# Splitting weights two blocks at a time, unscaled, with the norms' gains moved to the activations

## The chip, the core and the metric

The kernel runs on one core of a Trainium2 chip. That core has a matrix engine (TensorE, here PE), three engines for elementwise work (VectorE or DVE, ScalarE or ACT, GpSimd or POOL), a queue for transfers (SyncE or SP) and 16 DMA engines. An engine runs its instructions in the order in which they stand in its queue and waits on semaphores for the others. The metric is the time of one execution on the device in microseconds; the median of three runs before the change is 967.39 us (966.79 to 967.49).

## The reference

A trunk of two layers works on 256 tokens of 1024 features in float32. Each layer has three sub-layers, and each sub-layer has a root-mean-square norm before it and another behind it:

```python
for l in range(DEPTH):
    f = swiglu(rms_norm(x, ffn1_pre_g[l]), ffn1_w_gu[l], ffn1_w_down[l])
    x = x + 0.5 * rms_norm(f, ffn1_post_g[l])
    m = hybrid_mixer(rms_norm(x, mix_pre_g[l]), mix_w_in[l], mix_w_out[l], ...)
    x = x + rms_norm(m, mix_post_g[l])
    f = swiglu(rms_norm(x, ffn2_pre_g[l]), ffn2_w_gu[l], ffn2_w_down[l])
    x = x + 0.5 * rms_norm(f, ffn2_post_g[l])
```

`swiglu` multiplies by a 1024 x 5632 matrix, forms silu(g) * u and multiplies by a 2816 x 1024 one. `hybrid_mixer` multiplies by a 1024 x 2566 matrix; the result goes through three groups of heads (a gated linear recurrence, a Mamba-2 state space model in two chunks of 128 tokens, called SSD, whose result is normed with a gain of its own, `ssd_norm_g`, and a causal gMLP), and their 1024 columns are multiplied by `mix_w_out`. A norm is `rms_norm(x, g) = x * rsqrt(mean(x*x) + eps) * g`. The gain `g` belongs to a feature, that is, to a row of the weight that follows.

## The kernel before

**Products.** Every float32 operand of a main product is split into a high part (rounded to the type float32r of the language) and a low part (operand minus high part). A product is three matmuls, high x high, high x low and low x high, into one PSUM bank. `mm3` (L420) issues the three with 512 (or 390) weight columns as the moving operand and 128 tokens as the stationary one; `b_tile` (L692) issues them with 128 weight columns stationary and all 256 tokens moving.

**Weights.** All weights come in one packed stream. A unit is one block of 128 rows and up to 512 columns; there are 656 of them, in the order of use (`weight_units`, L51). Units are loaded in chunks of four (the first three chunks have one, one and two) into three staging buffers over SP's queue (`dma_chunk`, L339). A unit is then split (`split_next`, L383): ACT writes the high part and DVE the low part into a slot of two times 512 columns. There are 17 slots of kind "w"; a few general ones of kind "a" (13 in all) may be lent to the weights when a sub-layer allows it (`extra`). A unit's slot comes free with its last product (`release`, L413).

**Gains.** The pre-norm's gain is multiplied into the weight during the split, since a gain belongs to a weight row and a row to a partition: a unit that follows a norm is split by L400 (ACT, with a scale) and L401 (DVE, multiply and subtract), another by L396 and L397. So the norm's operand is x itself, transposed. `1 / rms` goes to the results. The same is done with `ssd_norm_g` for three of the eight row blocks of `mix_w_out`.

**From one sub-layer to the next.** `post` (L533) takes a token tile's two result banks: squares on ACT, gain on DVE (into tiles `s_f`, of which there are three), `1 / rms` by a power on POOL, and x is brought up to date on DVE. `pre` (L569) then makes the next operand for that token tile in two halves: four transposes on PE into a bank, a cast to the high part on ACT, a subtraction for the low part on DVE (tile `nT`). Down-products of the last four (or five) row blocks are held back, so that the first token tile ends earlier and its `post` and `pre` run beside the second tile's last products. In the first block of a sub-layer the first token tile's products come before the second's.

**What sets the order.** The program is written by a planner. It steps along PE's main products with a clock of its own for every engine (`T`), in which each operation costs a fixed part and a part by columns. The side computations are generators (`Chain`, L110), whose operations are issued when the planner holds their inputs to be due; all helpers of a chain issue at L137. `fill` (L364) issues splits of weights whenever DVE and ACT are due within 0.6 us and a slot is free. Thus every edit of an operation's cost can change the order of all engines' queues. `keep` pins the order of the first 15 us.

**Mixer.** Its first 16 units are the columns for dt and z (390 wide) and for the gMLP (512); then come groups of 384 or 512 columns for gates, recurrence, B and C, and x of the SSD; the out-product is last. `ssd_chunk` (L1092) norms the SSD's result without its gain, transposes it, and `split_out` (L869) writes the two parts.

Of the kernel before, what the change touches and what calls it, by code (L numbers as in the profile page):

```python
# [23 lines left out]
NSLOT = 17  # L24
NSCR = 13
# [25 lines left out]
def weight_units():  # L51
    units = []

    def add(name, l, blocks, scale=None):
        units.append((name, l, blocks, scale))

    def ffn(l, w):
        gu, dn, pg = f"ffn{w}_w_gu", f"ffn{w}_w_down", f"ffn{w}"
        for b in range(5):
            for off in (0, DFF):  # L60
                for k in range(KT):
                    add(gu, l, [(k * P, off + b * 512, 512)], (pg, k))
        for k in range(KT):
            add(gu, l, [(k * P, 2560, 256), (k * P, DFF + 2560, 256)], (pg, k))
        for k in range(DKT):
            for n in range(2):
                add(dn, l, [(k * P, n * 512, 512)])

    for l in range(DEPTH):
        ffn(l, 1)  # L70
        for k in range(KT):
            add("mix_w_in", l, [(k * P, C_DT, 6), (k * P, C_Z, 384)], ("mix", k))
        for k in range(KT):
            add("mix_w_in", l, [(k * P, C_UV, 512)], ("mix", k))
        for grp in FGROUPS:
            for k in range(KT):
                add("mix_w_in", l, [(k * P, c, P) for _, _, c in grp], ("mix", k))
        for k in OUT_KTS:
            for n in range(2):
                add("mix_w_out", l, [(k * P, n * 512, 512)], ("norm", k - 3) if 3 <= k < 6 else None)  # L80
# [4 lines left out]
def weight_chunks(units):  # L85
# [6 lines left out]
    return chunks  # L92

# [16 lines left out]
class Chain:  # L110
    """A side computation: a generator whose operations are issued when their inputs are due."""
# [110 lines left out]
class Kernel:  # L222
    def __init__(self, ctx, tc, x, wts, pf, pb, gpost, wst, wri, out):
# [20 lines left out]
        self.chunks = weight_chunks(self.units)  # L244
        self.u2c = {}
# [12 lines left out]
        self.wt, self.wh, self.wready, self.slot_time = {}, {}, {}, {}  # L258
        self.extra, self.keep_free = 0, 4

    # ---------------------------------------------------------------- memory
# [30 lines left out]
    # ---------------------------------------------------------------- issue order  # L292
# [25 lines left out]
    def wait_for(self, cond):  # L318
        while True:
# [4 lines left out]
            if self.next_split < len(self.units):  # L324
# [13 lines left out]
    # ---------------------------------------------------------------- weights  # L338
# [18 lines left out]
    def fill_time(self):  # L357
        d = self.next_split
        ci, _ = self.u2c[d]
# [4 lines left out]
    def fill(self):  # L364
        did = False
        while self.next_split < len(self.units):
            d = self.next_split
            ci, _ = self.u2c[d]
# [14 lines left out]
    def split_next(self, kind):  # L383
        d = self.next_split
        nc, T = self.nc, self.T
        u = self.units[d]
        w = unit_width(u)
        ci, o = self.u2c[d]
        src = self.ctile[ci][:, o:o + w]
        t, h = self.get([P, 2, 512], F32R, kind)  # L390
        hi, lo = t[:, 0, :w], t[:, 1, :w]
        sc = u[3] is not None
        T["act"] = max(T["act"], self.carrive[ci], self.slot_time.get(h, 0.0) + HOP) + 0.095 + w * 0.000833 + 0.095 * sc
        T["dve"] = max(T["dve"], T["act"] + HOP) + 0.07 + 0.06 * sc + w * 0.00104
        if not sc:
            self.keep(nc.scalar.copy(hi, src))  # L396
            self.keep(nc.vector.tensor_tensor(out=lo, in0=src, in1=hi.bitcast(F32), op=ALU.subtract))  # L397
        else:
            s = self.pcol(u[1], u[3][0], u[3][1])
            self.keep(nc.scalar.activation(hi, src, AF.Copy, scale=s))  # L400
            self.keep(nc.vector.scalar_tensor_tensor(out=lo, in0=src, scalar=s, in1=hi.bitcast(F32),  # L401
# [797 lines left out]
```

## Time and profile before

| | |
|---|---|
| median of the runs | 967.39 us (966.79 to 967.49) |
| span of the profiled execution, first to last instruction | 963.5 us |
| median less span | 3.9 us |
| PE busy | 945.1 us, 98% |
| DVE busy | 649.1 us, 67% |
| ACT busy | 580.4 us, 60% |
| POOL busy | 40.1 us, 4% |
| granted PE clock, mean | 0.998 |
| read from HBM | 173.57 MB, 181 GB/s over the span |

The profiled execution has no other time of its own than its span; what lies around the span is taken from the timed runs. Groups are named by line, engine, operation and tiles (written <- read). `acc` is a PSUM bank, `s_w` a weight slot, `s_a`, `s_m` and `s_f` are general tiles, `stg` is a staging buffer, `pf` the table of gains and other columns. PEld is PE's loading of stationary operands. The windows give for each stretch its length, the busy time of PE, PEld, DVE, ACT and POOL with the number of instructions, the granted clock, the share of the DMA engines' time and GB/s. With one line chosen, a window gives that line's busy time alone. In the timeline a row begins with start and length; in square brackets is idle time ahead of it and what ended it.

### The profile page before, as it was taken

The page shows a single profiled execution, that of the slowest core. Times are in us where ns is not written, and L with a number is a line of the kernel's source. Part 1 is how long each engine was busy: PE and PEld are TensorE (multiplying, and loading weights), DVE is VectorE, ACT ScalarE, POOL GpSimd, SP SyncE. Part 2 cuts the span into 40 slices and gives each one's busy share as a digit, 9 for nine tenths or more (in the row PEclk, how much of TensorE's full clock was granted, in tenths as well). Part 3 has the DMA queues.
Part 4 walks back from the last instruction along what each step waited for, and adds up shares of the span by engine and source line. Part 5 has one row for each costly group of instructions (what it writes and reads, how often), then busy time and mean ns, then how long its engine had stood idle before and what let it go on. Part 6 is the DMA issues. An engine that isn't in the chain of part 4 may idle for free.

```text
span 963.5 us, 16052 instructions
## 1 busy us (share of the span) xinstructions
PE 945.1 (98%) x6292; PEld 862.9 (90%) x6292; DVE 649.1 (67%) x1169; ACT 580.4 (60%) x1057; POOL 40.1 (4%) x58
## 2 busy tenths in 40 slices
PE   7999999999999999999999999999999999999997
PEld 6999998889986999998889999888999779999885
DVE  5876666566899856676565666666588996566632
ACT  7865555576967765555564555555589685454531
POOL 1100000001001100000010000000010110000000
PEclk9999999999999999999999999999999999999999
DMA  8855555443246945566435555663431566455621
GB/s 309 290 202 205 188 208 208 154 168 116 88 136 212 327 165 175 176 218 221 172 130 198 175 183 209 221 224 113 177 127 45 206 231 236 137 193 210 214 80 44
DMA packets 26717, 175.66 MB, mean 182 GB/s; under 512 B 2960, under 2 KB 3344, under 8 KB 7824
## 3 DMA queue, kind: packets, MB, share of 16 engines
q1 hardware_dynamic: 24768, 169.93, 50.0%
q10 hardware_dynamic: 1872, 4.70, 1.4%
q8 instruction: 49, 0.80, 0.3%
q14 instruction: 28, 0.23, 0.1%
HBM read 173.57 MB, written 1.05 MB: 181 GB/s over the span
## 4 chain that ended last, share of the span: by engine, by line
PE 89%; DVE 6%; ACT 2%; POOL 1%; issue 1%; DMA 0%; DVEq 0%; POOLq 0%; ACTq 0%
PE acc L704 46%; PE acc L425 39%; PE acc L137 4%; DVE s_w L401 2%; DVE s_a L137 1%; ACT s_a L137 1%; DVE x L137 1%; DVE s_f L137 1%; POOL postr L137 1%; DVE nT L137 1%; ACT L137 1%; POOL rs L137 0%; DMA x<-in_x_dram 0%; ACT junk L137 0%; POOL lnr L137 0%
## 5 line engine op out<-in xcount | busy, mean ns | idle before, releaser
L704 PE MATMUL acc<-nT,s_w 128*128 128x256 f32 x3900 | 467.5, 279 | 0.0
L704 PEld LDWEIGHTS acc<-nT,s_w 128*128 128x128 f32 x3900 | 460.3, 188 | 0.7
L401 DVE SCALAR_TENSOR_TENSOR s_w<-stg,pf,s_w 128x512 fp32r<-128x512 f32 (+2 forms) x435 | 299.2, 735 | 112.8 <-ACT s_w L400 112.5
L400 ACT ACTIVATE s_w<-stg,pf 128x512 fp32r<-128x512 f32 (+2 forms) x435 | 279.4, 701 | 113.7 <-PE acc L704 62.1
L425 PE MATMUL acc<-s_w,s_a 128*128 128x512 f32 x984 | 227.4, 390 | 0.0
L425 PEld LDWEIGHTS acc<-s_w,s_a 128*128 128x128 f32 x984 | 184.1, 188 | 37.9
L397 DVE TENSOR_TENSOR s_w<-stg,s_w 128x512 fp32r<-128x512 f32 x184 | 121.9, 687 | 61.9 <-ACT s_w L396 61.7
L396 ACT CAST s_w<-stg 128x512 fp32r<-128x512 f32 x184 | 107.0, 619 | 68.6 <-PE acc L425 36.7
L425 PE MATMUL acc<-s_w,nT 128*128 128x512 f32 (+1 forms) x522 | 129.3, 394 | 1.2 <-DVE nT L137 1.0
L425 PEld LDWEIGHTS acc<-s_w,nT 128*128 128x128 f32 x522 | 95.7, 189 | 21.6 <-DVE nT L137 2.3
L137 ACT ACTIVATE s_m<-s_m 128x512 f32<-128x512 f32 x36 | 22.6, 632 | 79.9 <-DVE s_m L137 79.9
L137 DVE TENSOR_TENSOR s_m<-acc,s_m 128x512 f32<-128x512 f32 (+1 forms) x64 | 35.7, 562 | 31.3 <-PE acc L704 25.8
L425 PE MATMUL acc<-s_w,s_m 128*128 128x512 f32 x192 | 48.0, 399 | 0.0
L425 PEld LDWEIGHTS acc<-s_w,s_m 128*128 128x128 f32 x192 | 34.8, 188 | 7.0 <-ACT s_m L137 0.5
L137 POOL TENSOR_TENSOR postr<-postv,mhalf 128x1 f32<-128x1 f32 x12 | 10.7, 893 | 705.7 <-DVE postv L137 705.7
L137 ACT CAST s_a<-s_m 128x512 fp32r<-128x512 f32 x36 | 22.1, 615 | 27.4 <-DVE s_m L137 26.9
L137 DVE TENSOR_TENSOR s_f<-acc,gp 128x512 f32<-128x512 f32 x24 | 16.5, 687 | 32.9 <-ACT junk L137 32.9
L137 ACT ACTIVATE junk<-acc 128x512 bf16<-128x512 f32 x24 | 14.2, 594 | 38.7 <-PE acc L425 38.2
L137 DVE TENSOR_TENSOR s_m<-acc,rb 128x512 f32<-128x512 f32 x36 | 24.7, 687 | 14.4 <-PE acc L704 14.4
L137 DVE TENSOR_TENSOR s_a<-s_m,s_a 128x512 fp32r<-128x512 f32 x36 | 24.7, 687 | 10.0 <-ACT s_a L137 10.0
L137 DVE SCALAR_TENSOR_TENSOR s_a<-s_f,pf,s_a 128x255 f32<-128x255 f32 (+2 forms) x60 | 28.5, 496 | 3.9 <-ACT s_a L137 3.9
L704 PE MATMUL acc<-nT,s_a 128*128 128x256 f32 x180 | 26.8, 279 | 0.0
(130 smaller groups left out, 526.0 us busy)
## 6 DMA issues: line engine op xcount, KB each, us to landing
stg<-in_wts_dram SPq DMA_DIRECT2D x147, 1024.0 KB, 5.0
stg<-in_wts_dram SPq DMA_DIRECT2D x12, 768.0 KB, 4.3
stg<-in_wts_dram SPq DMA_DIRECT2D x4, 780.0 KB, 4.4
gp<-in_gpost_dram ACTq DMA_DIRECT2D x6, 512.0 KB, 5.7
x<-in_x_dram SPq DMA_DIRECT2D x2, 512.0 KB, 4.4
out_dram<-x SPq DMA_DIRECT2D x4, 256.0 KB, 2.0
pb<-in_pb_dram ACTq DMA_DIRECT2D x2, 265.0 KB, 5.2
stg<-in_wts_dram SPq DMA_DIRECT2D x2, 256.0 KB, 4.6
```

Source lines behind the costliest of these rows:

```text
L137: ins = fn(*args, **kw)
L396: self.keep(nc.scalar.copy(hi, src))
L397: self.keep(nc.vector.tensor_tensor(out=lo, in0=src, in1=hi.bitcast(F32), op=ALU.subtract))
L400: self.keep(nc.scalar.activation(hi, src, AF.Copy, scale=s))
L401: self.keep(nc.vector.scalar_tensor_tensor(out=lo, in0=src, scalar=s, in1=hi.bitcast(F32), op0=ALU.mult, op1=ALU.subtract))
L425: self.keep(mm(out, a, b, start=start and i == 0, stop=stop and i == 2))
L704: self.keep(self.nc.tensor.matmul(out, a, b, start=k == 0 and i == 0, stop=k == KT - 1 and i == 2))
```

## The change

A group is two neighbouring units of a chunk (`split_groups`); the first two units, which have chunks of their own, are groups of one. `split_next` splits a whole group with one ACT copy and one DVE subtraction of up to 1024 columns, and never scales. High and low part have a slot of 1024 columns each, so a group takes two slots; 16 "w" slots stand in place of 17, and 14 "a" in place of 13, all of the same size. A group's slots come free when both units have had their last product. The gain of a pre-norm goes to the transposed x: `pre` multiplies the transposes by a column of gains, spread over 128 tokens, into an `s_f` tile, and the two parts are made from that. `ssd_norm_g` goes to the transposed result of the SSD, as a scale in the two operations of `split_out`.

```diff
-NSLOT = 17
-NSCR = 13
+NSLOT = 16
+NSCR = 14
...
+def split_groups(chunks):
+
+    return [c[i:i + 2] for c in chunks for i in range(0, len(c), 2)]
...
-        if self.free_slots["w"]:
+        if len(self.free_slots["w"]) > 1:
             return "w"
-        if self.extra > 0 and len(self.free_slots["a"]) > self.keep_free:
+        if self.extra > 1 and len(self.free_slots["a"]) > self.keep_free + 1:
             return "a"
...
-            lead = d - self.cur
+            lead = g[0] - self.cur
...
-                self.extra -= 1
+                self.extra -= 2
...
     def split_next(self, kind):
...
-        t, h = self.get([P, 2, 512], F32R, kind)
-        hi, lo = t[:, 0, :w], t[:, 1, :w]
...
-        if not sc:
-            self.keep(nc.scalar.copy(hi, src))
-            self.keep(nc.vector.tensor_tensor(out=lo, in0=src, in1=hi.bitcast(F32), op=ALU.subtract))
-        else:
-            s = self.pcol(u[1], u[3][0], u[3][1])
-            self.keep(nc.scalar.activation(hi, src, AF.Copy, scale=s))
-            self.keep(nc.vector.scalar_tensor_tensor(out=lo, in0=src, scalar=s, in1=hi.bitcast(F32),
-                                                     op0=ALU.mult, op1=ALU.subtract))
-        self.wt[d], self.wh[d], self.wready[d] = t, h, T["dve"]
+        w = unit_width(self.units[g[0]])
+        n = w * len(g)
+        ci, o = self.u2c[g[0]]
+        src = self.ctile[ci][:, o:o + n]
+        (th, h0), (tl, h1) = (self.get([P, 1024], F32R, kind) for _ in range(2))
+        hi, lo = th[:, :n], tl[:, :n]
+        free = max(self.slot_time.get(h, 0.0) for h in (h0, h1))
+        T["act"] = max(T["act"], self.carrive[ci], free + HOP) + 0.095 + n * 0.000833
+        T["dve"] = max(T["dve"], T["act"] + HOP) + 0.07 + n * 0.00104
+        self.keep(nc.scalar.copy(hi, src))
+        self.keep(nc.vector.tensor_tensor(out=lo, in0=src, in1=hi.bitcast(F32), op=ALU.subtract))
+        for i, d in enumerate(g):
+            self.wt[d] = (th[:, i * w:(i + 1) * w], tl[:, i * w:(i + 1) * w])
+            self.wh[d], self.wready[d] = (self.next_split, h0, h1), T["dve"]
+        self.left[self.next_split] = len(g)
...
     def release(self, d):
         del self.wt[d]
-        h = self.wh.pop(d)
-        self.slot_time[h] = self.now()
-        self.put(h)
+        g, *hs = self.wh.pop(d)
+        self.left[g] -= 1
+        if self.left[g] == 0:
+            for h in hs:
+                self.slot_time[h] = self.now()
+            self.put(*hs)
...
     def pre(self, t, nxt, halves):
...
-            yield from c.split(512, hi, lo, ps.rearrange("p (k s) -> p k s", k=4))
+            xg, h = yield from c.get([P, 4, P], F32, "f")
+            g = self.pcol(l, gain, 4 * q, 4).unsqueeze(2).to_broadcast([P, 4, P])
+            yield from c.tt(512, xg, ps.rearrange("p (k s) -> p k s", k=4), g, ALU.mult)
             c.free_aux(tag)
+            yield from c.split(512, hi, lo, xg)
+            self.put(h)
...
     def split_out(self, c, k, t, src, gain=None):
...
+            yield from c.act(P, o[:, 0, sl], src, AF.Copy, scale=gain)
+            yield from c.stt(P, o[:, 1, sl], src, gain, o[:, 0, sl].bitcast(F32), ALU.mult, ALU.subtract)
```

More of the change, by code (lines that the diff above doesn't have):

```diff
@@ L71, in weight_units @@
         for k in range(KT):
-            add("mix_w_in", l, [(k * P, C_DT, 6), (k * P, C_Z, 384)], ("mix", k))
+            add("mix_w_in", l, [(k * P, C_DT, 6), (k * P, C_Z, 384)])
         for k in range(KT):
-            add("mix_w_in", l, [(k * P, C_UV, 512)], ("mix", k))
+            add("mix_w_in", l, [(k * P, C_UV, 512)])
         for grp in FGROUPS:
             for k in range(KT):
-                add("mix_w_in", l, [(k * P, c, P) for _, _, c in grp], ("mix", k))
+                add("mix_w_in", l, [(k * P, c, P) for _, _, c in grp])
         for k in OUT_KTS:
             for n in range(2):
-                add("mix_w_out", l, [(k * P, n * 512, 512)], ("norm", k - 3) if 3 <= k < 6 else None)
+                add("mix_w_out", l, [(k * P, n * 512, 512)])
         ffn(l, 2)
@@ L244, in __init__ @@
         self.chunks = weight_chunks(self.units)
+        self.groups = split_groups(self.chunks)
         self.u2c = {}
@@ L258, in __init__ @@
         self.wt, self.wh, self.wready, self.slot_time = {}, {}, {}, {}
+        self.left = {}
         self.extra, self.keep_free = 0, 4
@@ L323, in wait_for @@
             times = [s[1] for s in self.chains if not callable(s[1])]
-            if self.next_split < len(self.units):
+            if self.next_split < len(self.groups):
                 times.append(self.fill_time())
@@ L357, in fill_time @@
     def fill_time(self):
-        d = self.next_split
-        ci, _ = self.u2c[d]
+        ci, _ = self.u2c[self.groups[self.next_split][-1]]
         if self.slot_kind() is None:
@@ L365, in fill @@
         did = False
-        while self.next_split < len(self.units):
-            d = self.next_split
-            ci, _ = self.u2c[d]
+        while self.next_split < len(self.groups):
+            g = self.groups[self.next_split]
+            ci, _ = self.u2c[g[-1]]
             while self.next_dma <= min(ci + NSTG - 1, len(self.chunks) - 1):
@@ L434, in a_step @@
         st = tuple(self.nT[:, i, k, t * P:(t + 1) * P] for i in range(2))
-        self.mm3(bk[0][:, :w], st, (wt[:, 0, :w], wt[:, 1, :w]), start, stop)
+        self.mm3(bk[0][:, :w], st, wt, start, stop)
     def setup(self):
@@ L569, in pre @@
     def pre(self, t, nxt, halves):
-        kind, _, ph = nxt
+        kind, l, ph = nxt
         xt = self.x[t]
+        gain = ("ffn1", "mix", "ffn2")[ph % 3]
         for q in range(2):
@@ L700, in b_tile @@
             w = self.unit(d + k)
-            wh, wl = (w[:, i, col:col + P] for i in range(2))
+            wh, wl = (w[i][:, col:col + P] for i in range(2))
             xh, xl = self.nT[:, 0, k, :], self.nT[:, 1, k, :]
@@ L867, in sgu, with split_out @@
         c.free_aux(at)
-    def split_out(self, c, k, t, src):
+    def split_out(self, c, k, t, src, gain=None):
         o = self.mixT[k][0]
         sl = slice(t * P, (t + 1) * P)
-        yield from c.split(P, o[:, 0, sl], o[:, 1, sl], src)
+        if gain is None:
+            yield from c.split(P, o[:, 0, sl], o[:, 1, sl], src)
+        else:
+            yield from c.act(P, o[:, 0, sl], src, AF.Copy, scale=gain)
+            yield from c.stt(P, o[:, 1, sl], src, gain, o[:, 0, sl].bitcast(F32), ALU.mult, ALU.subtract)
         c.flag(("mixT", self.phase, k, t))
@@ L1058, in ssd @@
         self.put(h_xw, h_bt, M["xs_h"])
-        yield from self.ssd_chunk(c, 1, xdt, xd)
+        yield from self.ssd_chunk(c, l, 1, xdt, xd)
         yield from c.until(("mixT", ph, 5, 0))
@@ L1090, in ssd_inputs, with ssd_chunk @@
         c.flag(("xin", ph, ch))
-    def ssd_chunk(self, c, ch, xdt, xd):
+    def ssd_chunk(self, c, l, ch, xdt, xd):
         M, ph = self.M, self.phase
@@ L1113, in ssd_chunk @@
         for f in range(3):
-            yield from self.split_out(c, 3 + f, ch, ps[:, f * P:(f + 1) * P])
+            yield from self.split_out(c, 3 + f, ch, ps[:, f * P:(f + 1) * P], self.pcol(l, "norm", f))
         c.free_aux(tag)
@@ L1159, in pack @@
         for u in c:
-            name, l, blocks, _ = units[u]
+            name, l, blocks = units[u]
             for r, col, n in blocks:
```

23 lines of the change are left out of this document (8 added, 15 removed).

## The prediction

> **What bounds the kernel now.** I read the page's first part, then the groups by line, then busy time stage by stage, then the chain of waits and the timeline at the two places where TensorE (PE) is short of work.
>
> ```profile
> span 963.5 us, 16052 instructions
> PE 945.1 (98%) x6292; PEld 862.9 (90%) x6292; DVE 649.1 (67%) x1169; ACT 580.4 (60%) x1057; POOL 40.1 (4%) x58
> ```
>
> PE is idle for 963.5 - 945.1 = 18.4 us in all. Matmuls overlap in the records, so a busy PE could still be a slow one; two pieces of the chain of waits (start, us, what) tell its pace.
>
> ```profile
> 37.27 97.43 PE acc L704 x835
> 134.69 54.46 PE acc L425 x240
> ```
>
> 97.43 / 835 = 0.1167 us for 256 columns, 54.46 / 240 = 0.227 us for 512. These stretches have no holes, and the change leaves the number and shape of the main matmuls alone: in them nothing can be won. Now the stages (window, length, busy us of each engine):
>
> ```profile
> 0.00:11.00 11.00, 5.67 (x21) 4.53 (x21) 3.55 (x7) 6.36 (x12) 1.17 (x10) 1.00 0.74 257
> 33.00:134.70 101.70, 101.70 (x873) 101.70 (x873) 70.88 (x124) 60.17 (x99) 0.00 (x0) 1.00 0.58 203
> 189.00:196.00 7.00, 6.63 (x34) 5.26 (x33) 5.60 (x10) 6.52 (x13) 0.99 (x1) 1.00 0.00 0
> 227.00:246.00 19.00, 17.90 (x145) 17.46 (x144) 14.65 (x37) 15.31 (x36) 4.03 (x6) 1.00 0.38 134
> 246.00:265.00 19.00, 18.84 (x158) 18.39 (x157) 16.02 (x41) 18.36 (x41) 0.00 (x0) 1.00 0.17 56
> 265.00:288.00 23.00, 23.00 (x124) 19.21 (x122) 21.89 (x49) 13.76 (x31) 1.54 (x2) 1.00 0.41 139
> 288.00:308.00 20.00, 18.74 (x85) 13.48 (x84) 17.65 (x34) 16.03 (x37) 4.65 (x5) 1.00 0.52 168
> 956.00:964.00 8.00, 0.71 (x4) 0.25 (x2) 2.24 (x4) 0.69 (x2) 0.55 (x1) 0.67 0.18 66
> ```
>
> PE idle: 5.33 us at the start, 7.29 at the end (the last norm and the store; no weight is split there), 0.37 where a swiglu hands over to the next sub-layer, and in one mixer with what follows it 1.10 + 0.16 + 1.26 = 2.52 us; the second layer repeats it. So about 5 us in the two mixers are all that a lighter VectorE (DVE) and ScalarE (ACT) can give. Everywhere else the change can only cost.
>
> **What splitting in pairs saves.** Groups (count | busy us, mean ns):
>
> ```profile
> L401 DVE SCALAR_TENSOR_TENSOR s_w<-stg,pf,s_w 128x512 fp32r<-128x512 f32 x377 | 264.4, 751 | 93.3 <-ACT s_w L400 93.3
> L397 DVE TENSOR_TENSOR s_w<-stg,s_w 128x512 fp32r<-128x512 f32 x184 | 121.9, 687 | 61.9 <-ACT s_w L396 61.7
> L137 DVE TENSOR_TENSOR s_a<-s_a,s_a 128x256 f32<-128x256 f32 x22 | 8.6, 415 | 0.0
> L137 ACT CAST s_m<-s_a 128x256 fp32r<-128x256 f32 x6 | 2.4, 402 | 0.0
> L396 ACT CAST s_w<-stg 128x512 fp32r<-128x512 f32 x184 | 107.0, 619 | 68.6 <-PE acc L425 36.7 <-DVE s_w L397 17.1 <-PE acc L704 14.8
> 296.65 3.17 ACT L400 ACTIVATE s_w<-stg,pf 128x512 fp32r<-128x512 f32 x5
> 303.24 2.65 DVE s_w L401 x4
> 302.04 1.20 DVE nT L137 x2
> ```
>
> In a row, a scaled split steps at 2.65 / 4 = 0.66 us on DVE and 3.17 / 5 = 0.63 on ACT; a plain 512-wide DVE operation steps at 1.20 / 2 = 0.60. The slopes are (687 - 415) / 256 = 1.06 ns a column on DVE and (619 - 402) / 256 = 0.85 on ACT. A 1024-wide one is not in the trace: by these, DVE steps at 0.60 + 512 x 1.06 ns = 1.14 us. For ACT the fixed part of one is 619 - 512 x 0.85 = 184 ns, some of it under its neighbour; it then steps between 0.87 (all hidden) and 1.05 us (none); I take 0.95. A scaled pair thus goes from 1.32 to 1.14 on DVE and from 1.27 to 0.95 on ACT; a plain pair gains 0.06 on DVE. There are 460 scaled units (4 swiglus of 88, 2 mixers of 54), hence 230 pairs: 41 us of DVE and 74 us of ACT, with some 6 us of DVE from the 98 plain pairs. All pairs have two units of one width, as each weight comes in runs of eight or more of a width, so the change does what it says. Nearly all of this lies under the gapless matmuls, where in 33 to 134.7 us DVE already rests 30% of the time: worth nothing there. Within a mixer (the splits of L401 alone, in a window of it):
>
> ```profile
> 217.00:246.00 29.00, 9.84 (x16) 1.00 0.38 132
> 237.59 0.99 DVE L401 SCALAR_TENSOR_TENSOR s_w<-stg,pf,s_w 128x384 fp32r<-128x384 f32 x1
> 238.90 0.61 DVE L401 SCALAR_TENSOR_TENSOR s_w<-stg,pf,s_w 128x384 fp32r<-128x384 f32 x1
> 239.83 0.61 DVE L401 SCALAR_TENSOR_TENSOR s_w<-stg,pf,s_w 128x384 fp32r<-128x384 f32 x1
> 241.41 0.41 DVE L137 TENSOR_TENSOR s_a<-s_a,s_a 128x256 f32<-128x256 f32 x1
> 241.97 0.41 PE L137 MATMUL acc<-ident,s_a 128*128 128x128 f32 x2 [1.10 <-DVE s_a L137]
> ```
>
> 16 units are 8 pairs, 1.4 us of DVE, of which at most the 1.10 + 0.16 = 1.26 us of PE idle there can be won. Most of it is here: PE stands 1.10 us at a transpose whose operand DVE makes behind three splits. Three of them take 2.2 us; as pairs 0.3 to 0.4 less, if their places in DVE's order stay. I take **-0.4 us a mixer, -0.8 in all**; the ends are -1.26 (all idle gone) and +0.6 (a second 1.14 us operation falls ahead, where one of half that size stood), a mixer.
>
> **What the moved gain adds.** Each of 24 quarters of the transposed x (6 sub-layers, 2 token tiles, 2 halves) gets a 512-wide DVE multiply out of PSUM ahead of the cast on ACT: 24 x 0.60 = 14 us of DVE, less than is saved. But it stands in series: transpose, multiply, cast, subtract, first product. It costs the 687 ns of `s_f<-acc,gp`, its like from PSUM (row below), and one more handover, about 0.1 us. The price of the chain is 0.8 us, at each place by its cover.
>
> ```profile
> L137 DVE TENSOR_TENSOR s_f<-acc,gp 128x512 f32<-128x512 f32 x24 | 16.5, 687 | 32.9 <-ACT junk L137 32.9
> 194.47 1.28 DVE L137 TENSOR_TENSOR nT<-acc,nT 128x512 fp32r<-128x512 f32 x2
> 195.23 0.86 PE L425 MATMUL acc<-s_a,s_a 128*128 128x512 f32 x3
> 195.93 0.69 PE L425 MATMUL acc<-s_w,nT 128*128 128x390 f32 x3
> ```
>
> *Swiglu to next sub-layer (three times).* The first low part is there at about 195.1; the other token tile's last down-products hold PE until 195.9, and the third product, which first reads it by now, falls near 196.3. Some 0.8 to 1.2 us of cover for 0.8 us: I take **+0.2 each, +0.6**; ends 0 and +1.3 (a 1.14 us split in front of the multiply or the subtract instead of a 0.66 one). The second token tile has the first tile's 48 products of 390 and 512 columns as cover, each over 0.17 us by the pace above: 8 us.
>
> ```profile
> 289.80 1.32 DVE s_w L401 x2
> 291.12 0.60 DVE s_f L137
> 293.79 1.29 PE L137 MATMUL acc<-ident,x 128*128 128x128 f32 x8 [0.87 <-DVE x L137]
> 294.46 0.59 ACT L137 CAST nT<-acc 128x512 fp32r<-128x512 f32 x1
> 295.09 0.96 PE L425 MATMUL acc<-s_w,nT 128*128 128x512 f32 x3
> 296.22 0.73 PE L425 MATMUL acc<-s_w,nT 128*128 128x512 f32 x2 [0.17 <-DVE nT L137]
> ```
>
> *Mixer to swiglu (twice).* Here PE has nothing left: it waits for x, then for the cast, then for the subtract. The multiply goes straight onto this path: **+0.8 each, +1.6**. Ends: -0.7 (the two splits that stand 1.32 us ahead of a post-norm step at 289.80 fall behind it, 1.32 against 0.8, and a little more), and +2.0 (the second half's multiply also comes first, and a 1.14 us split).
>
> ```profile
> 5.86 0.58 ACT L137 CAST nT<-acc 128x512 fp32r<-128x512 f32 x1 [3.10 <-PE acc L137]
> 7.77 0.69 DVE L137 TENSOR_TENSOR nT<-acc,nT 128x512 fp32r<-128x512 f32 x1
> 9.70 1.28 DVE L137 TENSOR_TENSOR nT<-acc,nT 128x512 fp32r<-128x512 f32 x2
> 11.04 0.73 PE L425 MATMUL acc<-s_w,nT 128*128 128x512 f32 x2 [0.64 <-DVE nT L137]
> ```
>
> *Start (once).* PE waits at 11.04 us for DVE. Of four multiplies the first fits before 7.1 us, where DVE is idle; about one and a half of the rest delay the third subtract. **+0.8 us**; ends +0.3 and +1.8 (all three, 3 x 0.60).
>
> The three norm columns of the mixer's output move from 6 weight units to 12 splits of 128 columns of the SSD result: a scalar operand in place of none costs 0.66 - 0.60 = 0.06 us on DVE, under out-products that leave PE no hole (23.00 of 23.00 us from 265 to 288); nothing, and 0.4 us for a tile's three splits, with ACT's share, if they were bare. Slots: 16 halves in place of 17 units hold 8 pairs, and two block-columns need 16 units, as before; the extra pairs in the "a" slots stay three. A pair's slot comes free one unit later, 3 to 6 products, under weights split a block ahead: nothing; at a handover that is the +0.5 in the upper ends. The DMA queue on SP issues the same chunks.
>
> **Sum:** -0.8 + 0.6 + 1.6 + 0.8 = +2.2 us on the span of 963.5, so 965.7. The median of the timed runs, 967.39, is 3.9 us over this span, for what lies around it; the same 3.9 gives 969.6.
>
> **The rivals.**
>
> *Covered.* DVE and ACT, lighter by some 33 and 74 us, reach each handover sooner, and what the multiply costs after the mixers (+1.6) comes back there: 0 to +1, median 967.9. For: DVE is busy 17.65 of 20 us at that handover. Against: half of what precedes the multiply there is the norm's own series, not splits.
>
> *Faster: the mixers' waits go.* In both layers the 2.52 us of PE idle between 227 and 308 us shrinks by three quarters, since the splits ahead of x and of the transposes take less of DVE or fall elsewhere in its order: -3.8, and the other terms near 0: 963.6. It decides from the point at which DVE's queue, not the series, holds the chain: the 1.32 us of splits at 289.80 speaks for it, the multiply against. The Trainium skill, Perfetto Trace Analysis, section Optimizing Scalar/DVE Operations, says that grouping into larger operations improves throughput if the engine is saturated; by that rule these stages, the only ones near saturation, gain.
>
> *Slower still: the coarse block.* In-order DVE can't put a norm's step ahead of a split under way, and a split now lasts 1.14 where it lasted 0.66: up to 0.5 us at two steps of each mixer's handover, one step of three others and the start, and at the 303.24 row's place before the next norm's factor: 6 x 0.5 + 3 x 0.5 + 0.5 = +5, with the +2.2 above a median of 974.6. The same section of the skill warns that where these engines aren't saturated but cause bubbles elsewhere, breaking instructions up lets work finish sooner; the change does the reverse, and 67% and 60% busy aren't saturation.
>
> **How the numbers follow.** Forecast 0.42 (its own range 968.2 to 971.5), covered 0.27, faster 0.19, coarse block 0.12. A measurement of this kernel tells about 0.2%, 1.9 us, from no change: 965.5 to 969.3 is "same". The forecast's lower part, 0.13, falls there with 0.23 of covered: same 0.36. Faster is 0.19 and 0.03 of covered: 0.22. Slower is 0.29 + 0.01 + 0.12 = 0.42. The range reaches to the faster case's 963.6, but not its whole, and to near the coarse block's: 963.8 to 974.0.
>
> **What would show it.** Right: a new multiply into an `s_f` tile between transpose and cast; PE's first product after each mixer later against its last down-product by 0.6 to 1.0 us; the first steady product at 11.5 to 12.5 us; the stretches at 0.1167 and 0.227 us unchanged; DVE near 616 us busy, ACT near 500. Wrong: PE idle in 227 to 308 us below 1.5 us (the faster rival), idle at the handovers unchanged (covered), waits of over a microsecond behind a 1024-wide split (coarse block), or any change of pace within the long stretches, which would upset the whole argument.

## The result and the profile after

The changed kernel takes 979.38 us (median; 978.95 to 980.88) against 967.24 before on the same chip: 1.0133 times the time, interval 1.012 to 1.0145, so some 12 us are lost where 2.2 were forecast. The profiled execution took 979.17 us for its span of 977.3. Only 1.9 us lay around it, not the 3.9 that the prediction took, so the execution profiled before was one of the quicker ones, and from span to span the loss reads 13.8. The stretches below are taken between these two profiles.

The page's first part after the change:

```profile
span 977.3 us, 15246 instructions
PE 948.0 (97%) x6292; PEld 865.2 (89%) x6292; DVE 610.0 (62%) x866; ACT 508.2 (52%) x732; POOL 43.5 (4%) x58
```

DVE lost 39 us of work and ACT 72, and the kernel became slower: PE is idle for 977.3 - 948.0 = 29.3 us instead of 18.4, and some of its busy time is slow. The groups of the splits (count | busy us, mean ns | idle before):

```profile
L402 DVE TENSOR_TENSOR s_w<-stg,s_w 128x1024 fp32r<-128x1024 f32 (+3 forms) x310 | 363.7, 1193 | 207.8 <-ACT s_w L401 207.2
L401 ACT CAST s_w<-stg 128x1024 fp32r<-128x1024 f32 (+3 forms) x310 | 305.9, 1024 | 213.0 <-PE acc L431 104.1 <-PE acc L716 92.0 <-DMA stg<-in_wts_dram 11.8
```

The places are found by numbering the main products as PE starts them and taking, for each, its start less the start of the same product before. What that delay grows by, in us, stretch by stretch (times of before, both layers together):

| | predicted | after |
|---|---|---|
| start, to 15.9 | +0.8 | -0.3 |
| three swiglu handovers (193.4-203.2, 477.2-495.9, 658.5-677.4) | +0.6 | +3.4 |
| mixers up to the out-product (203.2-267.0, 677.4-741.6) | -0.8, with the next row | +0.4 |
| out-product with the SSD (267.0-292.5, 741.6-767.1) | 0 | +6.5 |
| mixer to swiglu (292.5-324.5, 767.1-798.7) | +1.6 | +4.0 |
| all the rest | 0 | -0.1 |

Nearly half of it is in the stretch where the prediction saw PE without a hole. The windows of it and of the handover behind it (length, then busy us of PE, PEld, DVE, ACT, POOL, granted clock, DMA share, GB/s), after:

```profile
265.00:288.00 23.00, 21.20 (x115) 17.38 (x114) 22.33 (x40) 13.74 (x23) 2.04 (x2) 1.00 0.47 158
296.00:302.00 6.00, 2.87 (x15) 1.89 (x14) 5.99 (x11) 6.00 (x12) 1.80 (x2) 0.99 0.38 108
298.52:301.93 3.41, 0.74 (x5) 0.50 (x5) 3.41 (x6) 3.41 (x7) 1.18 (x1) 1.00 0.48 115
301.93:305.34 3.41, 3.41 (x9) 2.68 (x9) 2.97 (x6) 1.92 (x6) 1.22 (x2) 0.50 0.46 192
783.21:786.62 3.41, 2.88 (x7) 2.32 (x8) 3.41 (x7) 2.44 (x7) 1.15 (x2) 0.50 0.67 276
```

In the first PE has 1.8 us of idle time, and DVE is busy 22.33 of 23 us though its work over the whole kernel fell. In the second PE is idle half the time. The last three are the end of that gap and a spell at half the clock, once in each layer: eight matmuls start in the 3.41 us of the first one, where 0.227 us each would make fifteen.

**The out-product stage, row by row.** These are PE's waits in it after the change (start, length, what; in brackets the wait ahead of it):

```profile
270.51 0.83 PE L142 MATMUL acc<-ident,s_a 128*128 128x128 f32 x4 [0.37 <-ACT s_a L142]
271.87 4.17 PE L431 MATMUL acc<-s_w,s_m 128*128 128x512 f32 x17 [0.52 <-DVE s_w L402]
...
287.72 1.19 PE L431 MATMUL acc<-s_w,s_m 128*128 128x512 f32 x4 [0.91 <-ACT s_m L142]
289.48 0.52 PE L142 MATMUL acc<-ident,s_a 128*128 128x128 f32 x3 [0.58 <-DVE s_a L142]
```

Before, PE has no wait there. The second wait is for the low part of a weight itself; the last two are for the SSD's normed result and its split. By the delay of the products, 1.5 of this layer's 3.2 us are there by 270 us (times of before), and the rest comes between 282 and 286. DVE's timeline after:

```profile
271.73 0.48 DVE L142 SCALAR_TENSOR_TENSOR s_a<-s_f,pf,s_a 128x255 f32<-128x255 f32 x1
272.12 1.22 DVE L402 TENSOR_TENSOR s_w<-stg,s_w 128x1024 fp32r<-128x1024 f32 x1
273.25 0.48 DVE L142 SCALAR_TENSOR_TENSOR s_a<-s_f,pf,s_a 128x254 f32<-128x254 f32 x1
273.65 1.23 DVE L402 TENSOR_TENSOR s_w<-stg,s_w 128x1024 fp32r<-128x1024 f32 x1
...
276.31 0.56 DVE L142 TENSOR_TENSOR s_a<-acc,wdt 128x384 f32<-128x384 f32 x1
...
285.73 0.42 DVE L142 TENSOR_SCALAR s_a<-s_a,ynr 128x384 f32<-128x384 f32 x1
286.06 1.22 DVE L402 TENSOR_TENSOR s_w<-stg,s_w 128x1024 fp32r<-128x1024 f32 x1
287.20 0.14 DVE L142 TENSOR_SCALAR ynv<-yss 128x1 f32<-128x1 f32 x1
287.26 1.21 DVE L402 TENSOR_TENSOR s_w<-stg,s_w 128x1024 fp32r<-128x1024 f32 x1
288.92 0.42 DVE L142 TENSOR_SCALAR s_a<-s_a,ynr 128x384 f32<-128x384 f32 x1 [0.44 <-POOL ynr L142]
```

The same steps before:

```profile
270.39 0.47 DVE L137 SCALAR_TENSOR_TENSOR s_a<-s_f,pf,s_a 128x255 f32<-128x255 f32 x1
270.78 0.68 DVE L397 TENSOR_TENSOR s_w<-stg,s_w 128x512 fp32r<-128x512 f32 x1
271.38 0.47 DVE L137 SCALAR_TENSOR_TENSOR s_a<-s_f,pf,s_a 128x254 f32<-128x254 f32 x1
271.78 0.68 DVE L397 TENSOR_TENSOR s_w<-stg,s_w 128x512 fp32r<-128x512 f32 x1
...
273.98 0.55 DVE L137 TENSOR_TENSOR s_a<-acc,wdt 128x384 f32<-128x384 f32 x1
...
283.55 0.14 DVE L137 TENSOR_SCALAR ynv<-yss 128x1 f32<-128x1 f32 x1
...
284.36 0.42 DVE L137 TENSOR_SCALAR s_a<-s_a,ynr 128x384 f32<-128x384 f32 x1
```

Before and after, a split stands between one step of the convolution and the next, and again between steps of the SSD's norm. A split is now a pair: one step of the convolution follows the other in 273.25 - 271.73 = 1.52 us instead of 0.99. From the `wdt` step to the second chunk's multiply by `ynr`, the norm's factor, five splits stand in DVE's queue both times; they held five units before and ten now, and the way takes 12.6 us instead of 10.4. The out-products of the SSD's row blocks wait for that multiply.

The last two rows after show a second price: the multiply waits 0.44 us behind the split for POOL. These are POOL's two operations in the stage after, and, in a view by tile, all four of that kind before (least, median, most ns):

```profile
284.23 1.46 POOL L142 TENSOR_TENSOR ynr<-ynv,mhalf 128x1 f32<-128x1 f32 x1 [44.71 <-DVE ynv L142]
287.42 1.46 POOL L142 TENSOR_TENSOR ynr<-ynv,mhalf 128x1 f32<-128x1 f32 x1 [1.73 <-DVE ynv L142]
```
```profile
L137 POOL TENSOR_TENSOR ynr<-ynv,mhalf x4: 547/767/990, 280.4 to 758.3; 128x1 f32<-128x1 f32 x4
```

A power of one column takes 0.55 us at best and 1.46 beside a 1024-wide split: it ends 0.41 us after the split does (287.26 + 1.21 = 288.47, and 287.42 + 1.46 = 288.88; the other row and those of the halves further down give the same). With halves the multiply waits 0.44 us behind its split too; what the length adds is the split itself.

**The handover from mixer to swiglu.** From the chain of waits after (start, us, what):

```profile
296.85 0.76 DVE x L142
...
297.90 0.69 ACT junk L142 x2
298.59 0.93 ACT s_w L401
299.52 0.62 ACT junk L142 x2
300.15 0.94 ACT s_a L401
301.08 0.53 ACT nT L142
...
301.65 5.30 PE acc L431 x15
```

The cast of the transposed x stands behind two pairs' copies on ACT, 0.93 and 0.94 us. PE's timeline has the gap ahead of its first product, and the half clock begins 0.28 us behind it:

```profile
301.65 4.61 PE L431 MATMUL acc<-s_w,nT 128*128 128x512 f32 x12 [2.67 <-ACT nT L142]
```

The spells matter for the table. If half of PE's busy time in them is lost, (3.41 + 2.88) / 2 = 3.1 of the 4.0 us from mixer to swiglu are the clock's. This is an estimate, and so are the shares of the clock further down, made the same way from each run's spells.

### The profile page after: what moved, and what is told of

The parts are those of the page before. It is cut to its first block, busy times and chain, and to the rows that moved or that the text cites. A ratio compares the mean times of both kernels' runs of the same rounds, so it can differ in the third digit from the quotient of the medians.

```text
span 977.3 us, 15246 instructions
## 1 busy us (share of the span) xinstructions
PE 948.0 (97%) x6292; PEld 865.2 (89%) x6292; DVE 610.0 (62%) x866; ACT 508.2 (52%) x732; POOL 43.5 (4%) x58
## 3 DMA queue, kind: packets, MB, share of 16 engines
HBM read 173.57 MB, written 1.05 MB: 179 GB/s over the span
## 4 chain that ended last, share of the span: by engine, by line
PE 84%; DVE 10%; ACT 3%; POOL 1%; issue 1%; DMA 0%; DVEq 0%; POOLq 0%; ACTq 0%
PE acc L716 44%; PE acc L431 37%; DVE s_a L142 4%; PE acc L142 3%; DVE s_w L402 2%; DVE s_f L142 2%; ACT junk L142 1%; ACT s_a L142 1%; DVE x L142 1%; POOL postr L142 1%; DVE nT L142 1%; ACT L142 0%; DMA x<-in_x_dram 0%; POOL ynr L142 0%; DVE s_m L142 0%
## 5 line engine op out<-in xcount | busy, mean ns | idle before, releaser
L402 DVE TENSOR_TENSOR s_w<-stg,s_w 128x1024 fp32r<-128x1024 f32 (+3 forms) x310 | 363.7, 1193 | 207.8 <-ACT s_w L401 207.2
L401 ACT CAST s_w<-stg 128x1024 fp32r<-128x1024 f32 (+3 forms) x310 | 305.9, 1024 | 213.0 <-PE acc L431 104.1
L431 PE MATMUL acc<-s_w,s_a 128*128 128x512 f32 x960 | 222.1, 390 | 0.0
L431 PEld LDWEIGHTS acc<-s_w,s_a 128*128 128x128 f32 x960 | 179.6, 188 | 37.0
L431 PE MATMUL acc<-s_w,nT 128*128 128x512 f32 (+1 forms) x540 | 131.5, 397 | 6.3 <-ACT nT L142 5.9
L431 PEld LDWEIGHTS acc<-s_w,nT 128*128 128x128 f32 x540 | 101.7, 193 | 26.6 <-ACT nT L142 6.6
L142 DVE TENSOR_TENSOR s_m<-acc,s_m 128x512 f32<-128x512 f32 (+1 forms) x52 | 32.2, 624 | 38.6 <-PE acc L716 24.1
L431 PEld LDWEIGHTS acc<-s_w,s_m 128*128 128x128 f32 x192 | 35.0, 188 | 10.5 <-ACT s_m L142 2.3
L142 POOL TENSOR_TENSOR postr<-postv,mhalf 128x1 f32<-128x1 f32 x12 | 11.8, 981 | 729.7 <-DVE postv L142 729.7
L402 DVE TENSOR_TENSOR s_a<-stg,s_a 128x1024 fp32r<-128x1024 f32 (+1 forms) x19 | 22.7, 1195 | 9.6 <-ACT s_a L401 9.6
L401 ACT CAST s_a<-stg 128x1024 fp32r<-128x1024 f32 (+1 forms) x19 | 19.5, 1027 | 11.5 <-DMA stg<-in_wts_dram 11.5
```

The source lines that it names most:

```text
L142: ins = fn(*args, **kw)
L431: self.keep(mm(out, a, b, start=start and i == 0, stop=stop and i == 2))
```

## The experiments

A number taken from a stretch is the growth of the delay as in the table above, both layers together.

**One half of the change each.** First the moved gain with units split singly (17 and 13 slots, slots of `[P, 2, 512]`, released one by one):

```diff
-NSLOT = 16
-NSCR = 14
+NSLOT = 17
+NSCR = 13
...
-    return [c[i:i + 2] for c in chunks for i in range(0, len(c), 2)]
+    return [c[i:i + 1] for c in chunks for i in range(0, len(c))]
...
```

> One unit a split again (512 columns, one slot of two times 512, 17 and 13 slots), unscaled, and the gains on the transposed x and on the SSD's result as in the changed kernel: the moved gain alone. Theory A (the doubled split in DVE's order: one split stands between two steps of a chain whatever its length, so 25 units of weight instead of 16 come ahead of the mixer's last steps): near the kernel before, 967 to 970 us, the SSD and out-product stage as before, the multiply costing 0 to 3 us. Theory B (the multiply in series, with what it displaces, makes most of the loss): 976 to 980 us.

Then the pairs with the gain left on the weights, both units of a pair scaled by the first one's gain column, and no multiply in `pre`:

```diff
+            s = self.pcol(u[1], u[3][0], u[3][1])
+            self.keep(nc.scalar.activation(hi, src, AF.Copy, scale=s))
+            self.keep(nc.vector.scalar_tensor_tensor(out=lo, in0=src, scalar=s, in1=hi.bitcast(F32),
+                                                     op0=ALU.mult, op1=ALU.subtract))
...
-            yield from c.tt(512, xg, ps.rearrange("p (k s) -> p k s", k=4), g, ALU.mult)
```

> Pairs of 1024 columns as in the changed kernel, but scaled by a column of gains during the split (both units of a pair by the first one's gain, so the values of a pair's second unit differ from the reference's where the two rows differ), and no multiply on x or on the SSD's result: pairing alone. Theory A: 975 to 979 us, out-products waiting for the SSD as in the changed kernel. Theory B: 966 to 969 us.

Measured: the moved gain alone 974.61 us (971.44 to 979.70), ratio 1.0081 [1.005, 1.0111], between the two forecasts; the pairs alone 978.21, ratio 1.0123 [1.0108, 1.0138], as theory A has it. The pairs alone lose about as much as the whole change, and most of it in one place: 8.8 us in the out-product with the SSD, 2.0 at the swiglu handovers, 1.3 in the mixers before, and nothing (-0.2) from mixer to swiglu. Their splits, which scale, take 1.28 us instead of 1.22, and no spell at half the clock falls into their profile. The rows of PE that wait there, pairs alone:

```profile
287.71 0.52 PE L142 MATMUL acc<-ident,s_a 128*128 128x128 f32 x3 [0.68 <-DVE s_a L142]
...
291.02 0.52 PE L142 MATMUL acc<-ident,s_a 128*128 128x128 f32 x3 [1.17 <-DVE s_a L142]
```

These are the transposes of the SSD's normed result, waiting for DVE. The moved gain alone loses 0.4 there, 0.7 in the mixers before, 0.2 at the start, 0.6 at the three swiglu handovers, and from mixer to swiglu 3.2 in the first layer and 1.3 in the second. This is from its quickest run, which has no spell at half the clock either. Its waits at that place:

```profile
295.20 1.38 PE L142 MATMUL acc<-ident,x 128*128 128x128 f32 x8 [1.30 <-DVE x L142]
297.90 3.85 PE L432 MATMUL acc<-s_w,nT 128*128 128x512 f32 x14 [1.32 <-ACT nT L142]
...
327.45 0.66 PE L142 MATMUL acc<-ident,s_m 128*128 128x128 f32 x4 [1.85 <-DVE s_m L142]
```

The last row is the first layer's excess, in the next swiglu: PE waits 1.85 us for a step of DVE that stands behind four splits in a row. The timelines of DVE and POOL there:

```profile
322.60 4.20 DVE L403 TENSOR_TENSOR s_w<-stg,s_w 128x512 fp32r<-128x512 f32 x4 [1.27 <-ACT s_w L402]
```
```profile
322.95 1.62 POOL L142 COPY wbd<-s_f 64x384 f32<-64x384 f32 x2 [12.20 <-DMA s_f<-in_wri_dram]
324.65 1.60 POOL L142 TENSOR_TENSOR wst<-wst,tri 128x512 f32<-128x512 f32 x1
```

Four splits take 4.20 us there, 1.05 each instead of 0.60, beside POOL's work on the next layer's tables. The second layer has no such wait. The two halves give +7.5 and +11.1 on the medians, together 18.6, where the whole change costs 12.1: they are not additive. Without spells they aren't either: the two profiles lose 6.2 and 12.4 us of span, and the whole change 13.8, of which 3.1 are the clock's.

**Where must units be single?** Two runs mix single units with pairs in the changed kernel; a unit's number is taken within its layer's 328.

```diff
-    return [c[i:i + 2] for c in chunks for i in range(0, len(c), 2)]
+            one = 180 <= p[0] % 328 < 212
+            out += [[u] for u in p] if one else [p]
```

> The changed kernel, but the units of the out-product and the next swiglu's first 16 units are split one at a time (512 columns), unscaled; pairs everywhere else. Theory A: the SSD and out-product stage and the handover behind it lose their 5 us a layer, 969 to 973 us. Theory B: 977 to 980 us, as these units' splits aren't the cause.

```diff
+            r = p[0] % 328
+            one = r < 16 or 112 <= r < 212 or r >= 312
```

> The changed kernel with pairs only inside the swiglus: units are split one at a time from the last 20 of a swiglu, through the mixer, to the next swiglu's first 16. Theory A: what pairing costs lies at the mixers and handovers, so this comes near the kernel with single splits and the moved gain, 969 to 974 us. If it stays at 976 to 980 us, pairs cost something elsewhere (slots, prefetch).

Measured: 976.89 (ratio 1.0111 [1.0096, 1.0126]) and 975.73 (1.0097 [1.0078, 1.0116]); the first lies between its two forecasts and the second just below the upper one. With single units in the whole mixer the SSD stretch loses 2.2 instead of 6.5, but the handover behind it 8.4 instead of 4.0, 4.8 of this by the clock. With singles from unit 180 on the stretch still loses 5.9, though the splits that stand in it are 512 wide. Of this, 1.7 is a spell at half the clock that falls into the second layer's (768.75 to 772.16 us). Most of the rest is one wait of PE in each layer; these are the first layer's, and DVE's row ahead of it:

```profile
286.85 1.04 PE L148 MATMUL acc<-ident,s_a 128*128 128x128 f32 x6 [1.55 <-DVE s_a L148]
```
```profile
286.29 0.94 DVE L148 TENSOR_SCALAR s_a<-s_a,ynr 128x384 f32<-128x384 f32 x2 [0.44 <-POOL ynr L148]
```

POOL starts both chunks' powers in a row at 285.32 us, behind the second `ynv`, and both multiplies follow them, where before the first chunk's came 2.9 us ahead of the second's. Here the order of the steps goes with the loss, not the length of a split; what put it so is not settled.

**The planner's reach.** The planner puts in a split when DVE and ACT are due within `FILL`.

```diff
-FILL = 0.6
+FILL = 0.1
```

> The changed kernel with the planner's allowance FILL at 0.1 instead of 0.6 us: a split is put in only when DVE and ACT are due within 0.1 us by the planner's clocks, so fewer splits stand ahead of chain steps. Theory A: 972 to 977 us, with fewer units split ahead of the norm behind the mixer. Theory B: 978 to 980 us.

Measured: 985.92, ratio 1.0187 [1.0163, 1.0211]. That is slower than either forecast. The start alone loses 5.4 us, the mixers before the out-product 3.9, and the SSD stretch still loses 5.8, 1.7 of it by the clock. A shorter reach leaves fewer pairs ahead of the SSD's steps, but what that wins is lost elsewhere.

**The length of the operations.** DVE's subtraction of a pair in two of 512 columns, and then ACT's copy too, with slots and their release still by pairs:

```diff
-        self.keep(nc.vector.tensor_tensor(out=lo, in0=src, in1=hi.bitcast(F32), op=ALU.subtract))
+        for i in range(len(g)):
+            s = slice(i * w, (i + 1) * w)
+            self.keep(nc.vector.tensor_tensor(out=lo[:, s], in0=src[:, s], in1=hi[:, s].bitcast(F32), op=ALU.subtract))
```

> The changed kernel, but DVE makes a pair's low part in two operations of 512 columns, one behind the other (the planner's costs, slots, groups and ACT's 1024-wide copy as they are). Theory A (how many units of weight stand ahead of a chain's step in DVE's order): no gain, 978 to 981 us, since the same columns stand ahead. Rival C (the length of one DVE operation: the power on POOL took 0.55 us alone, 0.99 beside a 512-wide split and 1.46 to 2.07 beside a 1024-wide one, and it stands in each norm's series): powers of 1.0 instead of 1.5 us, and 974 to 977 us.

> The changed kernel with both operations of a pair, ScalarE's copy and VectorE's subtract, written as two of 512 columns, so that only the grouping of slots and their release by pairs is left of the pairing. If the length of the operations is what loses the 3.4 us a layer between 265 and 286 us, the loss there is at most 1.4 us (the value with the subtract alone in halves), the swiglu handovers cost 0.2 to 0.6 each, and the time is 972 to 976. If the pairs' common release of slots is what loses it, the 3.4 us stay and the time is 978 to 980. The multiply in series is still there, so below 971 neither holds.

Measured: 978.12 (1.0114 [1.0097, 1.013]) and 980.61 (1.0142 [1.0124, 1.016]). The SSD stretch answers as the theory of length has it: 2.6 and 2.7 us in place of 6.5, and with the subtraction in halves the powers on POOL are short again:

```profile
281.39 0.93 POOL L142 TENSOR_TENSOR ynr<-ynv,mhalf 128x1 f32<-128x1 f32 x1 [42.31 <-DVE ynv L142]
284.52 0.93 POOL L142 TENSOR_TENSOR ynr<-ynv,mhalf 128x1 f32<-128x1 f32 x1 [2.20 <-DVE ynv L142]
```

The time doesn't answer: mixer to swiglu now loses 6.2 and 9.6 instead of 4.0, so both forecasts of the total by the length (974 to 977, 972 to 976) are missed. Of this, 4.5 and 5.8 us are spells at half the clock, longer than the changed kernel's. The pairs' common release of slots is the same in these runs, so it is not what makes most of the 6.5 us. With both in halves the chain of waits there ends with two powers in series and a product that stands ahead of the main ones in PE's queue:

```profile
300.12 1.00 POOL postr L142
301.12 0.64 POOL rs L142
...
301.81 0.80 PE acc L142 x2
302.60 4.80 PE acc L433 x15
```

**Who sets the order.** The tiles' names carry a running number in the order in which the program was written. By a count from it, which the profiles don't show, 4 to 8 units that were written later stand ahead of the first layer's `postr` and norm steps on DVE in the changed kernel; before, 0 to 2 do. So the sentence further up, that the order is the planner's, holds for the first 15 us alone: behind them the language's own scheduling moves instructions when the kernel is built. One run capped the planner: no pair from the fifteenth unit of the out-product on before the SSD's last row block is written.

```diff
+            if self.cap is not None and self.cap[0] <= g[0] and self.cap[1] not in self.ready:
+                break
...
+        self.cap = (d + 14, ("mixT", ph, 5, 1))
```

> The changed kernel, but from the start of the mixer's out-product until the SSD's last part is written no unit beyond the 14th of the out-product may be split: 186 units' columns instead of 192 ahead of the second SSD norm (185 in the kernel before). Theory A: that step comes 2 to 3 us earlier in each layer, relative to the products before it, and unless the units put off are then late behind the mixer, 973 to 976 us. If the step is as late as in the changed kernel, the count of units ahead isn't the cause.

Measured: 980.99, ratio 1.0149 [1.013, 1.0168], and every engine's instructions stood in the same order as without the cap, so it decides nothing on the theory. It shows how far a stretch can move without any change of order: the SSD stretch loses 7.5 us instead of 6.5, and the handover behind it 5.2 instead of 4.0, by a longer spell at half the clock. Differences of a microsecond between the kernels below prove little. Three kernels then kept the written order: of everything after the change and before it, and of the splits alone after it.

```diff
-PIN = 15.0
+PIN = 1e9
```

> The changed kernel with every instruction kept in the order in which the planner wrote it (the limit of 15 us until which it does so is lifted); without that the language's own scheduler moves instructions, and in the changed kernel it puts 8 units of weight ahead of the second SSD norm, and 4 ahead of the norm behind the mixer, that the planner wrote behind them (2 and 0 in the kernel before). Theory D (these overtaking splits make the SSD and out-product stage late): that stage loses at most 1 us a layer and the whole is 968 to 974 us. If the planner's own order already holds the cause: 977 to 982 us.

> The kernel before with the planner's order kept throughout, as a reference for the pinned changed kernel. Theory D: little overtakes there (2 units at the SSD norms), so 964 to 970 us.

```diff
-        self.keep(nc.scalar.copy(hi, src))
-        self.keep(nc.vector.tensor_tensor(out=lo, in0=src, in1=hi.bitcast(F32), op=ALU.subtract))
+        self.keep(nc.scalar.copy(hi, src), True)
+        self.keep(nc.vector.tensor_tensor(out=lo, in0=src, in1=hi.bitcast(F32), op=ALU.subtract), True)
```

> The changed kernel with only the splits (ACT's copy and DVE's subtraction) kept behind what was written before them on their engine; other work may still be moved. Theory D: no unit overtakes a norm's step, so as with the whole order pinned or a little better, 967 to 974 us. If overtaking doesn't matter: 977 to 982 us.

Measured: 1022.32, 1013.04 and 986.68 us; ratios 1.058 [1.0564, 1.0596], 1.0491 [1.0466, 1.0516], 1.0216 [1.0199, 1.0233]. All three lie above their forecasts. The written order costs the kernel before 47 us, so the scheduling at the build is worth that much, and the change is slower without it too, by 9.3 us. With the splits alone kept, the SSD stretch loses 2.4 and the swiglu handovers 1.0, as a theory of splits that overtake has it; but the mixers before lose 5.3 and mixer to swiglu 12.0, 6.8 of it by the clock.

Put together: the units split between `wdt` and the second multiply by `ynr` in the first layer, the time of that way, what the SSD stretch and the handover behind it lose together in both layers, and what of this is the clock's (us):

| kernel | units | way | loss | by the clock |
|---|---|---|---|---|
| splits kept in written order | 4 | 9.9 | 14.5 | 6.8 |
| before | 5 | 10.4 | 0 | 0 |
| both operations in halves | 5 | 10.7 | 12.3 | 5.8 |
| low part in halves | 6 | 10.5 | 8.7 | 4.5 |
| reach of 0.1 us | 6 | 10.6 | 8.7 | 5.0 |
| moved gain alone | 6 | 11.1 | 4.9 | 0 |
| after, all in written order | 6 | 12.7 | 22.7 | 9.8 |
| pairs inside the swiglus only | 7 | 11.7 | 10.5 | 4.8 |
| before, with a truer price for the power (below) | 7 | 11.8 | -1.6 | 0 |
| single units from 180 on | 7 | 11.9 | 8.0 | 1.7 |
| before, all in written order | 7 | 13.1 | 15.7 | 5.6 |
| after | 10 | 12.6 | 10.5 | 3.1 |
| with the cap | 10 | 13.1 | 12.7 | 4.5 |
| pairs alone | 10 | 13.6 | 8.6 | 0 |

The way doesn't settle the loss: with the truer price it is longer than before by 1.4 us, and the SSD stretch itself loses 0.5. What a variant wins in the stretch comes back at the handover, and the clock has a large part in this. With the low part in halves, with both in halves and with the splits kept, the handover loses 2.2, 5.6 and 8.0 us more than after the change, and 1.4, 2.6 and 3.6 of these are the clock's. Whether the rest is splits that were not made in the stretch and are made at the handover instead, no run separates.

**A truer price for the power.** The planner holds a power on POOL to take 0.47 us; the rows show 0.55 to 0.99 before. In the kernel before, both powers' prices:

```diff
-        yield from c.op("pool", 0.47, self.nc.gpsimd.tensor_tensor, out=r, in0=v, in1=self.mhalf, op=ALU.pow)
+        yield from c.op("pool", 0.95, self.nc.gpsimd.tensor_tensor, out=r, in0=v, in1=self.mhalf, op=ALU.pow)
```

> The kernel before, with the norm factor's power on POOL priced at 0.95 us in the planner instead of 0.47, which is what it took beside a split: the transposes of x should no longer stand in PE's queue 0.5 us ahead of their operand at three handovers. 965 to 967 us if only that moves; the order of other work moves with it, so 963 to 971.

Measured: 965.30 us (965.05 to 966.20) against 966.78, ratio 0.9986 [0.9977, 0.9996]. It lies within the forecast and is the quickest of all kernels here; what it gains lies from mixer to swiglu (-2.1 us), part of it given back elsewhere.

## Why the prediction was wrong

The direction was right, but by the moved gain alone: the pairs, which make most of the loss, were forecast to help. The time, 969.6, was 9.8 us too low, and 979.38 lies above the range.

*The step that failed* is the price of the pairs: "**-0.4 us a mixer, -0.8 in all**". It was worked out from 217 to 265 us alone; the stretch behind that got no term for the pairs, and the little that the moved norm gain adds there was put at nothing because the out-products "leave PE no hole (23.00 of 23.00 us from 265 to 288)". The pairs alone cost 11.1 us by the medians, 12.4 from span to span, 8.8 of these in that very stretch. Two things were read wrongly. A stretch in which PE has no hole was taken for one with slack; DVE was busy there 21.89 of 23.00 us, in the row that the prediction quoted, and PE's products are fed by a series of DVE's steps. And the gain was worked out as three splits ahead of a step becoming shorter, "if their places in DVE's order stay". They don't stay: what stands in a gap between two steps is one split, whatever its length, so the step behind it is later by 0.53 us for each gap, and not earlier. That the length is the larger part of the cause in this stretch is shown: with the operations in halves 3.8 to 3.9 of the 6.5 us go, and single units throughout leave 0.4. It is not the whole: with singles from unit 180 on 4.2 us stay without the clock's share, 3.1 of them the two waits behind both chunks' multiplies.

*The multiply in series* was priced rightly at the swiglus and too low behind the mixers. With single units it cost 0.6 at the three swiglu handovers (predicted 0.6), and 1.2 and 1.3 from mixer to swiglu, without the wait of 1.85 us and what stands around it (predicted 0.8 each; the 1.2 is taken from 310 to 320 us). At the start it cost 0.2 where 0.8 was predicted, and after the whole change the start is even 0.1 to 0.3 earlier: the first steady product was to come at 11.5 to 12.5 us and came at 10.90, where it came at 11.04 before:

```profile
10.90 3.28 PE L431 MATMUL acc<-s_w,nT 128*128 128x512 f32 x13 [0.41 <-DVE nT L142]
```

That lies outside the term's bounds, whose lower end was +0.3; a gain at the start wasn't thought of.

*Together they cost more at the handovers*: 3.4 instead of 0.6 at the swiglus, 4.0 instead of 1.6 behind the mixers. Of the 4.0, 3.1 are the half clock, for which the prediction had no term at all; without it the stretch would lose some 0.9, less than was forecast. The pairs alone cost 2.0 and nothing there, and the multiply alone 0.6 and 2.5 without that wait. The rows from 296.85 us show the form: the series is one step longer, and each of its steps may meet a copy of 0.94 or a split of 1.14 us. What the interplay of order adds was seen, not taken apart.

*The rival "coarse block"* named the mechanism, and its bound, 974.6, was nearest. It gave up to 0.5 us a place, at handovers alone; the place that mattered, the gaps in the series of the convolution and the SSD, wasn't on its list. The Trainium skill's rule that was set beside it (Perfetto Trace Analysis, Optimizing Scalar/DVE Operations: breaking instructions up where these engines aren't saturated but cause bubbles) agrees with the halves' SSD stretch. The rule of the rival "faster", grouping where an engine is saturated, would have fitted this stretch by DVE's 21.89 of 23.00 us, and it lost there: by the rows above, the order of the steps and not the sum of DVE's work set the end.

Of the signs: DVE was to be near 616 us busy and was 610.0, ACT near 500 and was 508.2, and the pair's step, forecast at 1.14 and 0.95, is 1.13 and 0.93. Waits of over a microsecond behind a 1024-wide split, the coarse block's sign, came: the 2.67 us ahead of 301.65 stand behind two pairs' copies, though on ACT. PE's pace in the long stretches stayed; that a slower one could come at a handover, by the clock, wasn't foreseen. Open remain what sets the order of the SSD's steps and splits in each variant, and what of each variant's handover, beyond the clock, is work that moved there.

## What to carry to other kernels

Where side work is poured into the gaps of a series on an in-order engine, its grain is added to the series once for each gap. Lowering its total cost while doubling its grain can lose, and "busy all the time" on the engine that is fed says nothing about slack in what feeds it. Before pairing operations, count the gaps between the steps of the series on the engine that does both, and multiply by the difference in length. On the way above this gives 5 x 0.53 = 2.7 us, and it grew by 2.2. Then look at the clock of the matrix engine: a gap that leaves it mostly idle for 3.41 us cost up to 1.7 us more behind it. A planner's order is worth looking up in the queues as built, since a second scheduler may stand behind it.

## What the runs showed of the hardware

**A tiny operation on POOL waits out a long one on DVE.** A power of 128 x 1 took 0.55 us alone, 0.93 to 0.99 beside one 512-wide split, 1.46 beside a 1024-wide one, and 2.07 where an `nT` subtraction followed that at once (300.75 us after the change). Beside a multiply that takes one of its inputs from PSUM it stayed at 0.55 (202.23 us). The Trainium skill (SBUF — State Buffer, Who interferes with whom) says that a VectorE instruction with two SBUF inputs contends with a GpSimd instruction that reads SBUF, over a port pair that one holds to the other's exclusion; the rows agree. The prediction didn't weigh this rule: it makes every power on the path dearer by the split's growth.

**The clock falls in steps of 3.41 us.** After the change the granted clock is 0.50 from 301.93 to 305.34 us and from 783.21 to 786.62, each time following a stretch of 3.41 us with little work on PE (0.74 and 1.23 us busy of 3.41); each costs up to about 3.41 / 2 = 1.7 us, an estimate from the clock. Before, none occurs between the start and the end. With both operations in halves there are spells of 6.83 and 10.24 us. Counted in windows of 3.41 us that run on from the spells' edges, over the fourteen profiles, every window at full clock with less than 1.4 us of PE's time busy was followed by half the clock, and none with more than 2.1; between the two either happened. The moved gain alone lies between: in its profile, without a spell, the handover's two windows hold 2.0 us each, and its five runs took 971.44, 972.67, 974.61, 975.54 and 979.70 us at mean clocks of 0.998, 0.996, 0.996, 0.993 and 0.990. From the quickest to the slowest 0.008 / 0.5 of 980 us, some 15.7, are spent at half the clock in addition; half of that, 7.8 us, is nearly the whole difference of 8.3, an estimate. The Trainium skill (TensorE: Matmul & The Clock Gate, Part 1) describes a free-running window of this length and a half clock behind an idle one; the lengths agree, but a window need not be wholly idle.
